# Front of a hybrid GLA / Gated DeltaNet layer: the last segment of four chunks is split into two of two chunks

## The chip, the cores and the metric

The kernel runs on one core of a Trainium2 chip. The metric is device microseconds from the start to the end of one execution, as the median of several runs. The engines are named as in the profile: PE (TensorE), DVE (VectorE), ACT (ScalarE), POOL (GpSimd), and SP (SyncE), which issues most DMAs.

## The reference, cut to what matters

One decoder layer on 2048 tokens of width 1024: a token mixer with two head groups, an output projection with a layer norm, then a mixture of 64 experts with top-2 routing and a second layer norm. The change touches the mixer alone.

```python
proj = x @ w_in                                   # 1024 x 3608
qa, ka, va, ra, lra, qb, kb, vb, zb, bb, ab = split(proj)
gk  = log_sigmoid(lra @ w_gk_up + b_gk) / 16
o_a = rms_norm(gla_chunked(qa, ka, va, gk)) * silu(ra)
q, k, v = split(silu(causal_conv(concat(qb, kb, vb))))   # 4 taps along the sequence
beta, g = sigmoid(bb), -exp(a_log) * softplus(ab + dt_bias)
o_b = rms_norm(gdn_chunked(l2(q), l2(k), v, beta, g)) * silu(zb)
x1  = layer_norm(alpha * x + concat(o_a, o_b) @ w_out)
```

Both groups carry a state from chunk to chunk. The kernel uses chunks of 128 tokens, 16 in all.

## The kernel before, in words

The mixer has two parts. The front (`mixer_front`) works through the 16 chunks in segments, `SEGS` in line 320, each a pair of first chunk and number of chunks.

`project(si)` (lines 366 to 399) multiplies the segment's tokens by all of `w_in`. It first turns the tokens (PE transposes, line 378) and splits them into a high and a low part, `xhi` and `xlo`, of which there is one buffer each. Then it goes through 14 blocks of 256 to 272 columns of `w_in`. Every block is loaded in four pieces `raw` (line 390, issued by SP, three buffers), cast to `whi` on ACT (line 392), and subtracted to `wlo` on DVE and POOL in turn (line 393). Six blocks are token-major (line 412): per chunk 24 matmuls with 256 moving columns. Eight are channel-major (line 440): twice 24 matmuls whose moving columns are the tokens of the segment, 512 for four chunks. Six of these eight feed the causal convolution: ACT copies the tile from PSUM to `cr` (line 452, one buffer), POOL moves the three-token halo (lines 453 and 454), DVE makes four steps (lines 455 and 457), ACT a tanh (line 459) and DVE a last step (line 460). Results go to DRAM. The PSUM tiles of all this are called `mm`, and there are two.

The main loop (lines 734 to 747) calls for each segment `segment_gates` (once per segment: some 30 small DVE steps, `Gates.segment`), then for each chunk `load`, `gla_pre`, `gdn_prep`, `gla_post`, and for the chunk four before it `scan.chunk`, which is the serial part of the delta rule; after every fourth chunk comes `solve`, a triangular solve of four chunks on POOL (62 dependent steps, lines 688 and 690), and then the next segment's `project`. `scan.chunk` takes its PSUM from tiles named `p`, for chunks from 12 on from `mm` (line 743); it takes eleven one after the other. Its own buffers in SBUF (pool `p3work`) are single. `E` is a work tile with two buffers that `gla_pre`, `segment_gates` and `solve` share.

The loop is written in this order, but a planner sets the order on each engine. Work that stands earlier in the text has priority; later work, such as the next segment's projection, fills what is free. So `project(si + 1)` runs beside the chunks of segment `si`. Each engine then executes its own list in order. Almost all DMAs go through SP's list, one behind the other.

The second part, `mixer_out`, splits `w_out` into `wohi` and `wolo` (lines 881 and 882), in memory that the projection's ring used, runs the last four scans and projects chunk by chunk (transposes in line 907, matmuls in line 919). Its first transposes use the PSUM of `mm`. The experts and the last layer norm follow.

Of the kernel before, what the change touches and what calls it, by code (L numbers as in the profile page):

```python
# [316 lines left out]
KW, RB = 2, 3  # L317
LAG = 4
LEVELS = (64, 32, 16, 8, 4, 2, 1)
SEGS = ((0, 4), (4, 4), (8, 4), (12, 4))  # L320


def mixer_front(tc, nc, gt, scan, ident, x, w_in, conv_w, gla_g, gdn_g, w_gk, b_gk, dr):


    with ExitStack() as es:
# [39 lines left out]
        def project(si):  # L366
            c0, nch = SEGS[si]
            nt = nch * 128
# [96 lines left out]
        def segment_gates(si):  # L465
            c0, nch = SEGS[si]
            gt.segment(nc, work, ps, c0, nch)
            gs = work.tile([128, 4, 256], F32, name="gseg", bufs=1)
            u = work.tile([128, 2, 8, 128], F32, name="E").rearrange(
                "p a b c -> p (a b c)")[:, :1024].rearrange("p (a b) -> p a b", a=4)  # L470
            for j in range(nch):
                pz = ps.tile([128, 4, 128], F32, name="z", bufs=1).rearrange("p a b -> p (a b)")
                nc.tensor.transpose(pz[:16, 256:384], lra[:, si % 2, j, :], ident)
                nc.vector.tensor_copy(lT[j % 2][:16, :], pz[:16, 256:384])
                z = pz[:, :256]
                nc.tensor.matmul(z, lT[j % 2], wgk, start=True, stop=True)
                nc.vector.tensor_scalar(gs[:, j, :], z, 0.0, None, op0=OP.min)
                nc.vector.scalar_tensor_tensor(u[:, j, :], gs[:, j, :], -2.0, z, op0=OP.mult, op1=OP.add)
                T["g", c0 + j] = gs[:, j, :]
            gs, u = gs[:, :nch, :], u[:, :nch, :]  # L480
            nc.scalar.activation(u, u, AF.Exp, scale=-1.0)
            nc.scalar.activation(u, u, AF.Ln, bias=1.0)
            nc.vector.tensor_sub(gs, gs, u)
# [188 lines left out]
        def solve(seg):  # L672
            XR = work.tile([128, 2, 8, 128], F32, name="E").rearrange("p a b c -> p a (b c)")
            X = XR[:64, 0].rearrange("p (a b) -> p a b", a=32)
            for b in range(4):
                nc.gpsimd.dma_start(
                    X[16 * b:16 * b + 16],
                    flat(dr["na"], [[128 * 128, 16], [128, 32], [1, 32]],
                         seg * 16 * 128 * 128 + 32 * b * 129))
            R = XR[:64, 1].rearrange("p (a b) -> p a b", a=32)  # L680
            nc.gpsimd.memset(R, 0.0)
            nc.gpsimd.affine_select(R, R, pattern=[[1, 32], [-1, 32]], compare_op=OP.not_equal,
                                    fill=1.0, base=0, channel_multiplier=0)
            tmp = work.tile([128, 256], F32, name="stmp", bufs=1)
            for j in range(31):
                m, w = 31 - j, j + 1
                tv = tmp[:64, :m * w].rearrange("p (a b) -> p a b", b=w)
                nc.gpsimd.tensor_mul(tv, X[:, j, j + 1:, None].to_broadcast([64, m, w]),  # L688
                                     R[:, j:j + 1, :w].to_broadcast([64, m, w]))
                nc.gpsimd.tensor_add(R[:, j + 1:, :w], R[:, j + 1:, :w], tv)  # L690
            RT = X
            nc.scalar.activation(RT, R.rearrange("p a b -> p b a"), AF.Copy)
            for i, r in enumerate((R, RT)):
                for b in range(4):
                    nc.gpsimd.dma_start(
                        flat(dr["td"], [[4096, 16], [1, 1024]],
                             (i * NT + seg * 4) * 4 * 4096 + b * 1024),
                        r[16 * b:16 * b + 16].rearrange("p a b -> p (a b)"))
# [34 lines left out]
        nc.vector.tensor_copy(lm, lmf)  # L733
        for si, (c0, nch) in enumerate(SEGS):
            segment_gates(si)
            for c in range(c0, c0 + nch):
# [7 lines left out]
                if c % 4 == 3:  # L744
                    solve(c // 4)
            if si + 1 < len(SEGS):
                project(si + 1)
# [923 lines left out]
```

## Time and profile before

| | |
|---|---|
| runs of the kernel before | 2542.12, 2557.68 and 2557.61 us, median 2557.61 |
| profiled execution | 2542.03 us, span from first to last instruction 2540.0 us |
| mean granted TensorE clock | 0.98 of 2.4 GHz |
| busy share of the span | PE 95%, DVE 66%, ACT 44%, POOL 31% |
| front: first projection matmul to last scan | from 22 to 1094 us |
| output projection | from 1094 to 1391 us |

Times in the rows are microseconds from the start of the span, unless ns is said. "Busy" of an engine is the time in which at least one of its instructions is under way. Matmuls overlap their neighbours, so the duration of one is longer than the time between two of them.

A row of a window gives the stretch A:B, its length, then for PE, PEld (weight loads), DVE, ACT and POOL the busy time with the number of instructions, then the granted TensorE clock as a share of 2.4 GHz, the DMA share and GB/s. A window of one line has only that line's engines.

### The profile page before, as it was taken

To read this page: it belongs to the slowest core of one execution; us is meant where nothing else is said; L and a number is where in the kernel's file an instruction comes from. 1 tells how busy PE (TensorE), PEld (TensorE's weight loads), DVE (VectorE), ACT (ScalarE), POOL (GpSimd) and SP (SyncE) were. 2 spreads that over 40 slices of the span, in tenths; PEclk is the share of its full clock that TensorE was granted. 3 is DMA by queue.
4 is the path that set the end of the run, shared out by engine and by line. 5 is a ranking of instruction groups with operands and counts; after the bars stand their busy time and mean duration, and the time that the engine had idled before them with its cause. 6 is when DMAs were issued, how large, how long until landed. Compare 5 with 4: busy or idle time off the path is not lost.

```text
span 2540.0 us, 44666 instructions
## 1 busy us (share of the span) xinstructions
PE 2401.4 (95%) x16115; PEld 1794.8 (71%) x16115; DVE 1672.7 (66%) x3814; ACT 1114.7 (44%) x2202; POOL 794.6 (31%) x967
## 2 busy tenths in 40 slices
PE   7999989999999989889998999999989999999978
PEld 6797769887888778778877466766657667666543
DVE  6746884778577865878887366746645667465537
ACT  3435443554464444622222255645544556455422
POOL 5222582234832482274222111211111111121106
PEclk9999999999999999999999999999999999999989
DMA  5466446555654555645364999999999999999978
GB/s 164 127 188 189 121 112 190 183 150 162 215 175 134 162 174 168 208 128 191 112 235 145 401 408 420 372 401 406 406 409 384 409 407 407 398 400 409 403 284 341
DMA packets 268853, 679.33 MB, mean 267 GB/s; under 512 B 44436, under 2 KB 163798, under 8 KB 217302
## 3 DMA queue, kind: packets, MB, share of 16 engines
q1 hardware_dynamic: 252470, 639.04, 68.7%
q0 software_dynamic: 15744, 36.76, 4.1%
q8 instruction: 128, 2.10, 0.3%
q14 instruction: 95, 0.78, 0.1%
q10 hardware_dynamic: 416, 0.66, 0.1%
HBM read 591.91 MB, written 98.08 MB: 272 GB/s over the span
## 4 chain that ended last, share of the span: by engine, by line
PE 50%; DMA 18%; DVE 8%; issue 3%; ACT 3%; POOL 2%; DVEq 0%; SPq 0%; POOLq 0%; ACTq 0%
DMA w<-in_w_experts_dram 16%; PE gu L1354 14%; PE y L919 7%; PE mm L412 6%; PE y L1354 6%; PE mm L440 3%; PE ysum L1605 2%; DVE w L1218 2%; DVE oa L457 1%; PE misc L943 1%; POOL E L690 1%; PE xt L1355 1%; POOL stmp L688 1%; PE e L543 1%; ACT w L1217 1%
## 5 line engine op out<-in xcount | busy, mean ns | idle before, releaser
L1354 PE MATMUL gu<-w,xh 128*128 128x512 f32 (+1 forms) x2144 | 561.0, 495 | 19.3 <-DVE w L1218 9.4
L1218 DVE TENSOR_TENSOR w<-w,w 128x2048 fp32r<-128x2048 f32 x192 | 435.5, 2287 | 153.3 <-ACT w L1217 124.8
L1217 ACT ACTIVATE w<-w 128x2048 fp32r<-128x2048 f32 x192 | 364.5, 1914 | 199.6 <-PE gu L1354 80.5
L1354 PEld LDWEIGHTS gu<-w,xh 128*128 128x128 f32 (+1 forms) x2144 | 284.9, 166 | 229.3 <-issue 145.2
L1454 POOL DMA_INDIRECT y_d<-xg,ids x52 | 94.4, 1816 | 711.4 <-ACT w L1217 309.9
L1354 PE MATMUL y<-w,hh 128*128 128x512 f32 (+1 forms) x1072 | 280.4, 495 | 9.6 <-DVE w L1218 6.4
L412 PE MATMUL mm<-whi,xhi 128*128 128x256 f32 (+2 forms) x768 | 225.9, 294 | 2.4 <-DVE xlo L383 1.1
L440 PE MATMUL mm<-xhi,whi 128*128 128x512 f32 x512 | 210.3, 411 | 18.4 <-ACT cr L452 18.1
L412 PE MATMUL mm<-whi,xlo 128*128 128x256 f32 (+2 forms) x768 | 220.1, 287 | 0.0
L412 PE MATMUL mm<-wlo,xhi 128*128 128x256 f32 (+2 forms) x768 | 219.9, 286 | 0.0
L1354 PEld LDWEIGHTS y<-w,hh 128*128 128x128 f32 (+1 forms) x1072 | 141.1, 166 | 104.7 <-issue 67.3
L393 POOL TENSOR_TENSOR wlo<-raw,whi 128x512 fp32r<-128x512 f32 (+2 forms) x112 | 151.1, 1349 | 203.0 <-ACT whi L392 200.6
L440 PE MATMUL mm<-xlo,whi 128*128 128x512 f32 x512 | 208.3, 407 | 0.0
L392 ACT ACTIVATE whi<-raw 128x512 fp32r<-128x512 f32 (+2 forms) x224 | 132.5, 628 | 169.2 <-DMA raw<-in_w_in_dram 111.1
L440 PE MATMUL mm<-xhi,wlo 128*128 128x512 f32 x512 | 206.2, 403 | 0.0
L1354 PE MATMUL gu<-w,xl 128*128 128x512 f32 x560 | 176.7, 396 | 0.0
L393 DVE TENSOR_TENSOR wlo<-raw,whi 128x512 fp32r<-128x512 f32 (+2 forms) x112 | 103.0, 926 | 98.0 <-ACT whi L392 96.5
L412 PEld LDWEIGHTS mm<-whi,xhi 128*128 128x128 f32 x768 | 146.1, 190 | 7.5 <-DVE xlo L383 1.5
L412 PEld LDWEIGHTS mm<-whi,xlo 128*128 128x128 f32 x768 | 145.9, 190 | 2.3 <-issue 1.2
L412 PEld LDWEIGHTS mm<-wlo,xhi 128*128 128x128 f32 x768 | 146.1, 190 | 1.0 <-issue 0.2
L1451 DVE SCALAR_TENSOR_TENSOR xg<-y,gate,xg 128x512 f32<-128x512 f32 x104 | 74.6, 746 | 93.3 <-PE y L1354 93.0
L457 DVE SCALAR_TENSOR_TENSOR oa<-cr,cw,oa 128x512 f32<-128x512 f32 x144 | 131.6, 914 | 3.2
(461 smaller groups left out, 4623.8 us busy)
## 6 DMA issues: line engine op xcount, KB each, us to landing
w<-in_w_experts_dram SPq DMA_DIRECT2D x384, 1024.0 KB, 21.5
raw<-in_w_in_dram SPq DMA_DIRECT2D x192, 256.0 KB, 3.1
y<-y_d SPq DMA_DIRECT2D x16, 1024.0 KB, 18.3
bT_d<-oa SPq DMA_DIRECT2D x48, 256.0 KB, 2.4
bT<-bT_d SPq DMA_DIRECT2D x16, 768.0 KB, 5.6
xt<-in_x_dram SPq DMA_DIRECT2D x32, 256.0 KB, 4.0
qk<-bT_d SPq DMA_DIRECT2D x16, 512.0 KB, 4.2
x<-in_x_dram SPq DMA_DIRECT2D x16, 512.0 KB, 4.0
```

The source lines that it names most:

```text
L392: nc.scalar.activation(hi[:, ks, :n], raw, AF.Copy)
L393: (nc.gpsimd if h % 2 else nc.vector).tensor_sub(lo[:, ks, :n], raw, hi[:, ks, :n].bitcast(F32))
L412: nc.tensor.matmul(p[:, :n], xs[:, k, j * 128:(j + 1) * 128], ws[:, k, :n], start=(m == 0), stop=(m == 3 * KD - 1))
L440: nc.tensor.matmul(p, ws[:, k, s * 128:(s + 1) * 128], xs[:, k, :nt], start=(m == 0), stop=(m == 3 * KD - 1))
L457: nc.vector.scalar_tensor_tensor(o, r[:, w:w + nt], cw[:, w, b:b + 1], o, op0=OP.mult, op1=OP.add)
L919: nc.tensor.matmul(pf, a[:, k, :], w[:, k, cs], start=(m == 0), stop=(m == 3 * KD - 1))
L1217: self.nc.scalar.activation(full(hi), full(raw), AF.Copy)
L1218: self.nc.vector.tensor_sub(full(lo), full(raw), full(hi).bitcast(F32))
L1354: mm = lambda *args, **kw: tc.keep_in_program_order(nc.tensor.matmul(*args, **kw))
L1451: nc.vector.scalar_tensor_tensor(yt[:, cs], py[j], col.gate[:, c:c + 1], yt[:, cs], op0=OP.mult, op1=OP.add)
L1454: put = nc.gpsimd.indirect_dma_start(out=y_d, out_offset=bass.IndirectOffsetOnAxis(ap=col.ids[r, c:c + 1], axis=0), in_=yt[r], in_offset=N ...
L1605: keep(nc.tensor.matmul(p[:, cs], ident, ys[t][:, i, cs], start=(i == 0), stop=(i == 1)))
```

## The change

One line. The last segment, chunks 12 to 15, becomes a segment of chunks 12 and 13 and one of chunks 14 and 15. There are then five calls of `project`, the last two with 256 tokens each, and five of `segment_gates`; `project(4)` stands in the loop behind chunk 13 and before chunk 14. `solve` keeps its place behind every fourth chunk, and line 743 its limit of chunk 12.

```diff
--- before.py
+++ after.py
@@ -317,7 +317,7 @@
 KW, RB = 2, 3
 LAG = 4
 LEVELS = (64, 32, 16, 8, 4, 2, 1)
-SEGS = ((0, 4), (4, 4), (8, 4), (12, 4))
+SEGS = ((0, 4), (4, 4), (8, 4), (12, 2), (14, 2))
 
 
 def mixer_front(tc, nc, gt, scan, ident, x, w_in, conv_w, gla_g, gdn_g, w_gk, b_gk, dr):
```

## Rows read from the trace of the kernel before

**Rows 1.** The page, part 1: engine, busy us (share of the span), instructions.

```profile
PE 2401.4 (95%) x16115; PEld 1794.8 (71%) x16115; DVE 1672.7 (66%) x3814; ACT 1114.7 (44%) x2202; POOL 794.6 (31%) x967
```

**Rows 2.** Windows of the front, all engines (columns: see above).

```profile
454.00:715.00 261.00, 255.11 (x2404) 218.10 (x2391) 189.82 (x575) 131.12 (x411) 125.25 (x182) 0.99 0.60 181
715.00:988.00 273.00, 259.36 (x2474) 222.49 (x2472) 192.34 (x590) 126.98 (x398) 120.33 (x176) 0.95 0.52 153
988.00:1094.00 106.00, 91.85 (x1391) 73.91 (x1390) 85.00 (x365) 63.72 (x253) 31.55 (x53) 0.90 0.68 209
988.00:1042.00 54.00, 46.84 (x711) 37.87 (x714) 41.80 (x152) 34.92 (x126) 16.35 (x26) 0.87 0.78 244
1042.00:1094.00 52.00, 45.01 (x697) 36.05 (x684) 43.20 (x214) 28.80 (x129) 15.19 (x27) 0.93 0.58 172
```

**Rows 3.** The chain of waits, 840 to 990 us: start, length, what, how many.

```profile
917.37 19.44 PE mm L440 x72
...
972.81 3.03 PE mm L412 x24
```

**Rows 4.** Single lines: count: ns min/median/max, first and last start.

```profile
L845 PE MATMUL p<-gdn_s,qk x64: 275/275/275, 480.7 to 896.9; 128*128 128x128 f32 x64
...
L845 PE MATMUL mm<-gdn_s,qk x32: 275/288/421, 1016.6 to 1091.4; 128*128 128x128 f32 x32
...
L907 PE MATMUL mt<-ident,ma x64: 271/273/328, 1094.5 to 1352.0; 128*128 128x128 f32 x64
```

**Rows 5.** Windows of the channel-major line 440 and the token-major line 412 alone.

```profile
60.00:85.00 25.00, 24.24 (x103) 18.80 (x103) 1.00 0.43 123
842.00:936.00 94.00, 73.79 (x288) 54.97 (x289) 0.96 0.54 155
...
165.00:202.00 37.00, 35.87 (x288) 34.25 (x287) 1.00 0.58 176
```

**Rows 6.** Single lines 412 and 440.

```profile
L412 PE MATMUL mm<-whi,xlo x768: 274/283/689, 22.7 to 988.3; 128*128 128x256 f32 x128, 128*128 128x272 f32 x32, 128*128 128x264 f32 x32
...
L440 PE MATMUL mm<-xhi,whi x512: 387/393/796, 49.7 to 935.9; 128*128 128x512 f32 x171
```

**Rows 7.** Lines by form, 715:988 us: count | busy us, mean ns | idle before.

```profile
L392 ACT ACTIVATE whi<-raw 128x512 fp32r<-128x512 f32 x48 | 28.3, 626 | 30.7 <-DMA raw<-in_w_in_dram 20.1 <-PE mm L440 7.7 <-PE mm L412 2.7
...
L393 DVE TENSOR_TENSOR wlo<-raw,whi 128x512 fp32r<-128x512 f32 x24 | 21.3, 892 | 22.2 <-ACT whi L392 22.2
...
L393 POOL TENSOR_TENSOR wlo<-raw,whi 128x512 fp32r<-128x512 f32 x24 | 32.8, 1367 | 29.4 <-ACT whi L392 27.3 <-POOL att L574 1.1 <-ACT gu L286 1.0
```

**Rows 8.** Single lines of VectorE.

```profile
L457 DVE SCALAR_TENSOR_TENSOR oa<-cr,cw,oa x144: 730/752/2470, 58.4 to 924.2; 128x512 f32<-128x512 f32 x144
...
L424 DVE SCALAR_TENSOR_TENSOR st<-th,st x64: 404/426/1596, 28.4 to 989.7; 128x256 f32<-128x256 f32 x64
...
L293 DVE SCALAR_TENSOR_TENSOR gp<-gp,gs x7: 157/166/174, 820.3 to 825.1; 128x16 f32<-128x16 f32 x7
```

**Rows 9.** Single line 390, the weight loads on SP's queue, 715 to 988 us.

```profile
L390 SPq DMA_DIRECT2D raw<-in_w_in_dram x49: 368/383/777, 714.9 to 964.8; - x49
```

**Rows 10.** Windows of smaller stretches, columns as in rows 2.

```profile
715.00:744.00 29.00, 25.56 (x514) 22.05 (x512) 22.60 (x77) 16.14 (x51) 9.73 (x14) 0.82 0.54 161
...
842.00:875.00 33.00, 33.00 (x180) 26.12 (x179) 30.27 (x84) 17.27 (x54) 13.68 (x17) 1.00 0.53 160
883.00:941.00 58.00, 50.82 (x248) 40.81 (x247) 41.57 (x69) 24.02 (x50) 48.97 (x77) 0.94 0.54 160
```

**Rows 11.** Lines of VectorE in 842:875 and 883:941 us.

```profile
L457 DVE SCALAR_TENSOR_TENSOR oa<-cr,cw,oa 128x512 f32<-128x512 f32 x12 | 9.2, 765 | 0.1
...
L457 DVE SCALAR_TENSOR_TENSOR oa<-cr,cw,oa 128x512 f32<-128x512 f32 x12 | 14.8, 1232 | 0.1
```

**Rows 12.** Lines, 988 to 1094 us.

```profile
L882 DVE TENSOR_TENSOR wolo<-x,wohi 128x1024 fp32r<-128x1024 f32 x8 | 10.4, 1308 | 1.4 <-ACT wohi L881 1.4
```

## Prediction, written before the changed kernel ran

> **What bounds the kernel now.** I read the page's busy times first, then the windows of the front's stretches, then the chain of waits and single lines. TensorE is busy 95% of the span and VectorE 66% [rows 1], but those shares mix stages, and the change touches only the front (everything before the output projection), so it has to be read there. The windows cut the front where a projection's last matmul ends. The third segment's chunks with the last projection beside them take 273 us, and the last four chunks, with no projection left, 106 us [rows 2]. The change works on these 379 us. The reader is to see two things. First, the bare 106 us are not empty: TensorE is busy 91.85 of them, so 14.2 us are idle, at a mean granted clock of 0.90, against 0.95 and 0.99 in the stretches with a projection [rows 2]. The first half of them (chunks 12 and 13) idles 54 - 46.84 = 7.2 us at 0.87, the second half (chunks 14 and 15) 52 - 45.01 = 7.0 us at 0.93. Second, a projection does not come free beside chunks: 261 and 273 us go by with TensorE idle only 5.9 and 13.6 us [rows 2]. The time is the sum of both works, not the longer one. The chain inside the channel-major blocks goes through VectorE's convolution as well as TensorE (72 matmuls in 19.44 us, 0.27 us each, slower than when nothing holds them), and through TensorE alone in the token-major blocks (24 in 3.03 us) [rows 3]. The front ends with the scan: its four bare chunks read the state from 1016.6 to 1091.4 us, one per 25 us, and the output projection's first transposes follow at 1094.5 [rows 4].
>
> **The matmuls.** A projection has 8 channel-major blocks x 2 x 24 = 384 matmuls of 512 columns and 576 token-major ones. Two half projections have 768 of 256 columns instead of the 384, and the same 576. For the price I take instructions per time and not durations: 103 matmuls of 512 columns fill 24.24 us, 0.2353 us each; 288 of 256 columns fill 35.87 us, 0.1246 us each [rows 5]. So 768 x 0.1246 - 384 x 0.2353 = 95.7 - 90.4 = **+5.3 us**. The last token-major tiles, 24 in 3.03 us [rows 3], would make it +6.6; exact halving 0; I keep 0 to 7. The durations say otherwise: 283 ns against 393 ns [rows 6], and 768 x 0.283 - 384 x 0.393 would be +66 us. But neighbours overlap, as the counts per time show, so that is no price here. The Trainium skill (Trainium Kernel Development and Optimization, Performance Expectations) warns that matmul busy time misleads on how close a kernel is to its limit, because matmuls are pipelined. By the busy times the sum would be 61 us higher; the counts side with the Trainium skill.
>
> **Chunks 12 and 13 get cover.** Their 7.2 us of idle fall to the rate of the two covered stretches, (5.9 + 13.6)/534 = 3.7% of some 47 us, 1.7 us: **-5.5 us** (0 to -7.2). The clock: at 0.87, 2 x 0.13 x 54 = 14 us of that half ran at 1.2 GHz, at 0.97 it would be 3. Eleven microseconds at full pace save at most half, 5.5; but the scan's matmuls had a median of only 288 ns there against 275 elsewhere [rows 4], so I take **-2.5 us** (0 to -5.5). Chunks 14 and 15 stay bare, and their 7.0 us of idle stay.
>
> **A second pass over the input weights.** One more projection loads and splits all of them again, 14 blocks of 4 pieces: 56 ScalarE casts at 626 ns, 35 us; 28 subtractions on VectorE at 892 ns, 25 us; 28 on GpSimd at 1367 ns, 38 us [rows 7]. The convolution and its neighbours become twice as many half-width steps. The nearest row for a 256-wide three-operand step on VectorE is 426 ns, against 752 for 512 wide [rows 8], so 36 steps cost 36 x (2 x 426 - 752) = 3.6 us more, and the two steps around them some 2.4 more by the same ratio. A fifth round of gate arithmetic is 26 short steps like the 166 ns one [rows 8], 4.3 us. Together VectorE gets about 35 us more on 192.3 + 85.0 = 277.3 of 379 us [rows 2], which makes 82%. On SP's queue there are 56 more weight loads at 383 ns [rows 9], 21 us of issue, and each waits for a buffer of `raw` with the chunk loads, stores and scan loads queued behind it. All of it lies beside TensorE's work as long as the chunks fill TensorE; VectorE has run at 30.27 of 33 us, 92%, with TensorE not idle at all [rows 10]. Where the solve on GpSimd meets the convolution that cover is gone: 7.2 of 58 us idle [rows 10]. Twelve of the last projection's sixteen channel tiles took 94 us [rows 5]; sixteen at half the columns are 94 x 16/12 / 2 = 63 us, and 12.4% of that is **+7.8 us**. Bounds: 0 with full cover, +35 with none of VectorE's added time covered. I take the value by the solve row because project(4)'s channel blocks must start soon after that solve.
>
> GpSimd's added work has a second price. A convolution step takes 765 ns where GpSimd is lightly used and 1232 ns beside the solve [rows 11]. If all 38 us of added GpSimd work met such steps, they would lose 38 x (1 - 765/1232) = 14 us; that stands inside the bound above. The Trainium skill (GPSIMD Engine Reference, Key points) gives a reason against the change: GpSimd shares its SBUF interfaces with VectorE and contends with instructions that read two SBUF inputs. The two rows agree; without that rule the added GpSimd work would cost VectorE nothing.
>
> **One more start.** project(4) can write `xhi` only after project(3)'s last matmul, as every projection must. The last such start shows 25.56 of 29 us busy [rows 10]: 3.4 us idle, and chunks beside it. Half the tokens are turned each time, so no transpose is added. I take **+1.5 us** (0 to 3.4).
>
> **The output weights move.** The split of `w_out` needs memory of the projection's ring, so it now waits for project(4) and falls beside chunks 14 and 15. It is 8 VectorE subtractions, 10.4 us [rows 12], in a stretch where VectorE is already busy 43.2 of 52 us [rows 2]: 53.6 us of work. The output projection uses the slices one after the other, so only a part is late: **+3 us** (0 to 10.4).
>
> **Sum.** 5.3 - 5.5 - 2.5 + 7.8 + 1.5 + 3 = **+9.6 us**. On the profiled execution's 2542.0 us (span 2540.0) that is 2551.6. The runs shown stand at two levels, 2542.1 once and 2557.7 and 2557.6; with the profiled one their mean is 2549.9, and I put the change on that mean: **2559.5 us**. All the bounds together are -13 to +56, but the ends exclude each other: full cover goes with the gains, no cover with the losses. One per cent, about what a measurement of this kernel can tell from no change, is 25 us, so the forecast is no change.
>
> **Rivals.**
> *Slower: the scan loses its buffers.* For chunks from 12 on the scan takes its PSUM from `mm`, of which there are two. Before, no projection was left then; now project(4) takes from the same two, with 4 turns, 16 channel tiles and 12 token tiles against 11 takes per scan chunk. If scans 8 and 9 are put off until project(4) is through, four scans stand in the bare end, 4 x 25 = 100 us [rows 4], instead of 52. TensorE has then its 45 us of chunks 14 and 15 and some 16 of the two scans (an estimate, a third of 45), so 39 us are idle instead of 7: 32 us more, 2591.5. With one scan late it is half, 2575.5. It decides from the point where both scans stand behind project(4)'s last tile. For it: the scan is a serial chain, and bare it already sets the pace of 25 us. Against it: the covered scans between 480.7 and 896.9 us [rows 4] kept up in the planner's order. Chance 0.13.
> *A little faster: the solve moves off the convolution.* project(3) ends earlier, so the third solve may meet its token blocks and project(4)'s start instead of the channel blocks. Then the 7.2 us idle of 883 to 941 go away and +7.8 becomes -7.2: sum -5.4, 2544.5. For it: the solve hangs on chunk 11 alone. Against it: the solve is some 58 us long and project(4) begins inside it. Chance 0.17.
> *It does not do what it says.* Chunk 12 needs project(3)'s last blocks, the gates and an `E` buffer that the solve also holds; if chunks 12 and 13 therefore come mostly after project(4), the -5.5 and -2.5 are gone: +17.6, 2567.5. Chance 0.12.
> Forecast: 0.58.
>
> **How the numbers follow.** The forecast's own range is 2545.5 (both gains in full, feed and start at nothing: 5.3 - 7.2 - 5.5 + 3 = -4.4) to 2569 (the feed twice as dear and the start at 3.4: +19.3). Below lies the second rival on the lower of the two levels of the runs, above it the first: 2534 to 2586 leaves out most of the two-scan case. Slower by over 1% (above 2575) needs both scans late or most of the added VectorE time bare: 0.10 + 0.04 = 0.14. Faster by over 1% needs more than the 14 us of bare idle and clock that chunks 12 and 13 have to give: 0.03. The rest, 0.83, is no change.
>
> **What would show it.** The bare end, from the last projection matmul to the output projection, should be 50 to 60 us instead of 106, at a clock like 0.93. From 715 us to that point it should be some 325 to 340 instead of 273. VectorE busy in the whole stretch should be near 312 us and GpSimd 40 higher. The 256-column matmuls of the channel blocks should come about 0.125 us apart. If the four reads of the state in `mm` still lie 25 us apart and end 75 us after the first, with the first near the end of project(4), the first rival holds. A front that ends before 1080 us would mean that the feed is hidden; the time after the front should move with its end and not change by itself.

## The result and the profile after

The changed kernel takes 2661.84 us (median of 4 runs, 2656.95 to 2672.62), beside 2555.70 us for the kernel before (4 runs): a ratio of 1.043, 95% interval 1.038 to 1.047. It is 106 us slower where no change was forecast. The profiled execution after took 2656.95 us, its span 2655.1. The medians of the kernel before that were taken beside the experiments lie between 2547.83 and 2556.24 us, so a few microseconds between kernels of different experiments are not read as a difference.

Up to the end of the third projection both kernels run the same instructions in the same order. The profiled one after is 13.5 us later by then (726.7 against 713.2 us); the runs of the kernel before differ among themselves by as much. From there to the output projection's first transposes the kernel before takes 381.3 us and the changed one 478.6. What follows is nearly equal: 2540.0 - 1094.5 = 1445.5 us against 2655.1 - 1205.3 = 1449.8. So the whole loss lies in the stretch that the change touches. The page's first part, beside [rows 1], shows TensorE 46 us busier and GpSimd 40:

```profile
PE 2447.1 (92%) x16505; PEld 1846.9 (70%) x16505; DVE 1727.2 (65%) x3929; ACT 1155.1 (44%) x2295; POOL 834.4 (31%) x1019
```

Windows after, columns as in [rows 2]: the fourth projection beside chunks 8 to 11; then a stretch with no projection; the fifth projection; the bare end:

```profile
728.00:925.00 197.00, 176.97 (x2112) 159.98 (x2112) 155.00 (x524) 106.46 (x364) 82.00 (x119) 0.91 0.62 183
925.00:1028.00 103.00, 62.69 (x736) 49.67 (x735) 56.85 (x195) 34.96 (x133) 49.75 (x85) 0.67 0.34 103
1028.00:1151.00 123.00, 100.99 (x839) 94.52 (x839) 80.95 (x192) 57.53 (x141) 40.98 (x50) 0.94 0.56 163
1151.00:1205.00 54.00, 43.74 (x593) 34.96 (x592) 41.68 (x156) 30.72 (x109) 16.10 (x22) 0.84 0.64 206
```

The second line is the failure of the change's purpose. Most of chunks 12 and 13 still runs with no projection beside it: TensorE idles 40.3 of 103 us, and its granted clock is 0.67, two thirds of the time at 1.2 GHz. The third line is the other loss: half a projection, with the fifth round of gates and some work of chunk 14 beside it, takes 123 us, where the whole first one of the kernel before takes 181. The last line is the bare end for chunks 14 and 15, half as long as the 106 us of [rows 2].

The chain of waits after, 925 to 1155 us (start, length, what), tells why nothing covers the second line:

```profile
989.44 3.45 POOL td_d L695 x7
992.89 2.24 DMA td_d<-E
995.28 1.89 DMA td<-td_d
997.31 1.26 POOL tt L786
...
1025.20 1.71 PE mm L845 x8
1026.91 1.68 PE mm L769 x8
1029.06 3.62 DMA xt<-in_x_dram
```

And TensorE's waits in 925 to 1028 us (engine, line, what it waited for: us, times, longest):

```profile
PE mm L800 <- DMA td<-td_d: 13.8, 1, 13.8
PE e L543 <- DVE E L523: 10.0, 3, 6.8
```

Scan 8 takes its PSUM tiles from `mm` and waits for the third solve, which stores its result at 989 to 995 us. The `mm` tiles are handed out in the order of the program's text, and there scans 8 and 9 (called with chunks 12 and 13) stand ahead of the fifth projection. So its input load and transposes come directly behind scan 9's last matmuls at 1027 us, 102 us after the projection before it ended. The scan's reads in `mm` after, beside [rows 4]:

```profile
L845 PE MATMUL mm<-gdn_s,qk x32: 275/348/421, 1008.8 to 1203.6; 128*128 128x128 f32 x32
```

Before, the four reads lay within 75 us, behind all projections. Now two lie ahead of the last projection and two behind it, 195 us from first to last.

### The profile page after: what moved, and what is told of

Read it like the earlier page. It is cut to its first block, busy times and chain, and to the rows that moved or that the text cites. A ratio compares the mean times of both kernels' runs of the same rounds, so it can differ in the third digit from the quotient of the medians.

```text
span 2655.1 us, 45942 instructions
## 1 busy us (share of the span) xinstructions
PE 2447.1 (92%) x16505; PEld 1846.9 (70%) x16505; DVE 1727.2 (65%) x3929; ACT 1155.1 (44%) x2295; POOL 834.4 (31%) x1019
## 4 chain that ended last, share of the span: by engine, by line
PE 41%; DMA 25%; DVE 10%; ACT 4%; issue 3%; POOL 2%; SPq 0%; DVEq 0%; ACTq 0%; POOLq 0%
DMA w<-in_w_experts_dram 21%; PE gu L1354 11%; PE y L919 6%; PE mm L412 4%; PE y L1354 4%; PE mm L440 3%; DMA raw<-in_w_in_dram 3%; PE ysum L1605 2%; DVE w L1218 2%; DVE oa L457 1%; PE misc L943 1%; ACT whi L392 1%; DVE wlo L393 1%; POOL E L690 1%; PE xt L1355 1%
## 5 line engine op out<-in xcount | busy, mean ns | idle before, releaser
L393 POOL TENSOR_TENSOR wlo<-raw,whi 128x512 fp32r<-128x512 f32 (+2 forms) x140 | 189.2, 1352 | 290.6 <-ACT whi L392 289.8
L440 PE MATMUL mm<-xhi,whi 128*128 128x512 f32 (+1 forms) x640 | 238.8, 373 | 28.4 <-ACT cr L452 28.2
L392 ACT ACTIVATE whi<-raw 128x512 fp32r<-128x512 f32 (+2 forms) x280 | 166.9, 630 | 207.2 <-DMA raw<-in_w_in_dram 145.2
L440 PE MATMUL mm<-xlo,whi 128*128 128x512 f32 (+1 forms) x640 | 234.2, 366 | 0.0
L440 PE MATMUL mm<-xhi,wlo 128*128 128x512 f32 (+1 forms) x640 | 233.2, 364 | 0.0
L393 DVE TENSOR_TENSOR wlo<-raw,whi 128x512 fp32r<-128x512 f32 (+2 forms) x140 | 124.3, 893 | 110.2 <-ACT whi L392 107.8
L440 PEld LDWEIGHTS mm<-xhi,whi 128*128 128x128 f32 x640 | 127.9, 200 | 55.1 <-ACT cr L452 34.6
L440 PEld LDWEIGHTS mm<-xhi,wlo 128*128 128x128 f32 x640 | 128.2, 200 | 17.8 <-issue 0.2
```

Source lines behind the costliest of these rows:

```text
L392: nc.scalar.activation(hi[:, ks, :n], raw, AF.Copy)
L393: (nc.gpsimd if h % 2 else nc.vector).tensor_sub(lo[:, ks, :n], raw, hi[:, ks, :n].bitcast(F32))
L440: nc.tensor.matmul(p, ws[:, k, s * 128:(s + 1) * 128], xs[:, k, :nt], start=(m == 0), stop=(m == 3 * KD - 1))
```

## Experiments: the scans' buffers

**Scans 8 and 9 in p.** The changed kernel, where only the scans behind the last projection take `mm`:

```diff
-  name="mm" if c >= 12 else "p", bufs=2))
+  name="mm" if c >= 14 else "p", bufs=2))
```

(The `c` of this line is the chunk with which a scan is called, four ahead of its own: `c >= 12` is scan 8 onward. Where the expectations speak of scans 12 and 13, they mean those called with these chunks, scans 8 and 9.)

> The changed kernel with one number altered: the scan takes its PSUM from mm only for chunks 14 and 15, and from p for chunks 12 and 13. Theory A (the two mm buffers): in the changed kernel project(4) got its first mm tile only when scan 9 had taken its last, so it ran alone after chunks 12 and 13. Then project(4)'s transposes should start within some 20 us of project(3)'s last matmul, the bare end should stay near 54 us, and the time should fall from 2657 to 2550 to 2575 us (my forecast of +9.6 on before). Theory B (the second pass over the weights at half width is dear wherever it runs): the time stays above 2620 us, with project(4) still taking over 110 us for itself. Theory C (scan 8 waits for the third solve): the 13.8 us wait of TensorE for td stays and the time falls by less than 20 us.

Measured: 2614.37 us, ratio 1.024 (1.022 to 1.027). The fifth projection now starts 2 us after the fourth (927.0 after 924.8), and 47 us of the 106 are back. The time lies between the ranges of theory A (2550 to 2575) and theory B (above 2620): each has a part of the loss. The rest, some 60 us, is not a matter of this order. Windows of this kernel, and of the kernel before over the same stretch of work, from the third projection's end to the output projection:

```profile
725.00:1164.00 439.00, 370.50 (x4285) 329.38 (x4284) 336.73 (x1071) 231.41 (x749) 188.03 (x275) 0.90 0.59 177
```

```profile
713.00:1094.00 381.00, 353.21 (x3893) 297.93 (x3891) 278.11 (x956) 192.25 (x654) 152.16 (x229) 0.94 0.56 168
```

In 58 us more, TensorE is busy 17 us more and idle 41 us more (68.5 against 27.8), VectorE is busy 59 us more, GpSimd 36, ScalarE 39. The two largest of TensorE's waits in these stretches (us, times, longest), first here, then in the kernel before:

```profile
PE mm L440 <- ACT cr L452: 16.1, 8, 4.6
PE e L543 <- DVE E L523: 13.9, 7, 5.6
```

```profile
PE mm L440 <- ACT cr L452: 6.5, 2, 5.0
PE e L543 <- DVE E L523: 3.5, 5, 1.1
```

The first hangs on the convolution's buffer, the second on a step that VectorE makes for each chunk. Together they are 20 of the 41 us of added idle time; the rest is spread over many short waits.

**The same hole made in the kernel before.** Scan 4 onward takes `mm`, so that the whole last projection stands behind scan 7:

```diff
-  name="mm" if c >= 12 else "p", bufs=2))
+  name="mm" if c >= 8 else "p", bufs=2))
```

> The kernel before, segments of four, with the scan taking mm already for chunks 8 to 11. Theory A: project(3) now waits until scan 7 has taken its last mm tile, so chunks 8 to 11 run bare (some 106 us) and the whole project(3) alone (some 182 us) instead of both in 273 us: 15 to 30 us slower than before, 2560 to 2585, because a whole projection alone is not much slower than TensorE and the third solve lies beside it. If the loss of cover alone explains the changed kernel's 97 us, it should be 60 us or more here. Theory B: no projection is added, so no more than 10 us slower.

Measured: 2587.90 us, ratio 1.013 (1.011 to 1.016), 34 us slower. The last projection begins at 831.2 us, right behind scan 7, and its matmuls then take 182.5 us nearly alone. That is 3 us above theory A's range. Two `mm` tiles claimed too early cost 34 us with no half projection anywhere.

**A short third solve.** The changed kernel with 4 of the third solve's 31 steps; the other 27 are left out:

```diff
-  for j in range(31):
+  for j in range(4 if seg == 2 else 31):
```

> The changed kernel with the third solve cut to its first 4 of 31 steps (27 steps of the triangular solve for chunks 8 to 11 are left out, so later values differ, and only the front is read). Theory C (scan 8, and behind it project(4), wait for that solve on GpSimd): the wait for td goes away and the front ends 25 to 45 us earlier than in the changed kernel's 1205 us. Theory A alone, without the solve: it ends no more than 15 us earlier. Theory B: no change over 10 us.

Measured in one run: 2617.34 us; the output projection begins at 1167.6 instead of 1205.3 us, 38 us earlier, as theory C had it. TensorE's wait for `td` is gone, and the stretch without a projection shrinks from 101 to 53 us. This kernel also has less work on GpSimd, so the 38 us need not all come from the shorter wait. The loss is one chain, solve to scan 8, scan 9, `mm`, projection; broken at the first link it gives back 38 us, at `mm` 47.

## Experiments: what a projection of two chunks costs

**The first segment in two.** The kernel before, where `mm` has no other taker so early:

```diff
-SEGS = ((0, 4), (4, 4), (8, 4), (12, 4))
+SEGS = ((0, 2), (2, 2), (4, 4), (8, 4), (12, 4))
```

> The kernel before with the first segment of four chunks split into two of two, the last left whole; no scan runs there, so mm is free for the projection. Theory A (the two mm buffers are what costs): the second pass is then hidden beside chunks 0 and 1, and the time is 2542 to 2575 us. Theory B (half-width passes are dear by themselves): the first projection, alone and for two chunks, takes 115 us or more instead of half of the 182 us that a whole one alone takes, and the second one is as slow: 40 to 100 us slower than before, above 2590.

Measured: 2630.40 us, ratio 1.030 (1.028 to 1.032). So a second pass over the weights costs 77 us where no scan takes `mm`, within theory B's range. The first projection of two chunks, and the whole first projection of the kernel before:

```profile
15.00:143.00 128.00, 106.04 (x838) 99.33 (x837) 81.75 (x180) 59.10 (x135) 54.49 (x72) 0.91 0.60 178
```

```profile
22.00:203.00 181.00, 174.02 (x1098) 150.68 (x1099) 104.67 (x207) 67.69 (x144) 48.53 (x62) 0.99 0.52 152
```

Half the columns take 71% of the time. VectorE, ScalarE and GpSimd do 78%, 87% and 112% of a whole pass's work for them, since casts and subtractions of the weights don't get shorter. TensorE's waits in the two:

```profile
PE mm L440 <- ACT cr L452: 13.5, 10, 2.4
PE mm L412 <- DVE lra L426: 2.8, 1, 2.8
```

```profile
PE mm L440 <- ACT cr L452: 5.7, 3, 2.2
```

Ten pauses instead of three. Five of the ten were followed by a stretch at half clock; the other five, 0.3 to 2.4 us long, were not. Line 440 alone in e3_split_first, 2 us inside each of three tiles: the first follows a pause of 1.9 us, the second one of 0.3 and the third one of 2.4 (last columns: granted clock, DMA share, GB/s):

```profile
68.50:70.50 2.00, 2.00 (x11) 2.00 (x11) 0.50 0.72 222
72.00:74.00 2.00, 2.00 (x19) 2.00 (x19) 1.00 0.74 192
103.00:105.00 2.00, 2.00 (x20) 2.00 (x19) 1.00 0.62 152
```

By their start times a matmul of 256 columns follows the last after 0.21 us at 1.2 GHz and after 0.12 at 2.4.

**One shared cause after another.** Two theories for the pauses were a single `cr` buffer under the convolution, and weights that come late:

```diff
-  xt = ring.tile([128, 512], F32, name="xt", bufs=3)
+  xt = ring.tile([128, 512], F32, name="xt", bufs=2)
...
-  r = ring.tile([128, 515], F32, name="cr", bufs=1)
+  r = ring.tile([128, 515], F32, name="cr", bufs=2)
```

> The kernel before with its first segment as two of two chunks (as in e3_split_first, which took 2630.4 us), and a second cr buffer for the convolution; to make room, two xt buffers instead of three. Theory D (the convolution's chain over one cr buffer sets the pace of a projection of two chunks): in e3_split_first TensorE started a weight block of the convolution every 9.9 us (six of them in a pass of 128 us), where its 48 matmuls need 6.0 at 0.125 us; with a second buffer the pitch falls to what VectorE needs, 2 x (0.43 + 3 x 0.59 + 0.63) + 2 x 0.84 = 7.3 us, so 2.5 us x 12 blocks = 30 us less: 2600 (2590 to 2612). Theory F (the weights arrive too late: three raw buffers, the DMA, the split): no change, 2625 to 2635. Theory V (VectorE's own work sets the pace): 2620 to 2632.

Measured: 2612.34 us, ratio 1.023 (1.019 to 1.026): 18 us less, 30 expected, at the upper end of theory D's range. The waits for `cr` go from 13.5 to 7.4 us in the first pass, and a wait of 6.5 us for `oa` takes some of their place.

With `RB = 4` in place of the second `cr`:

> The kernel before with its first segment as two of two chunks (as in e3_split_first, 2630.4 us), and four raw buffers for the weights instead of three; two xt buffers instead of three. Theory D (the convolution's one cr buffer): within 8 us of 2630. Theory F (the weights arrive too late; in the first pass ScalarE waited 27.1 us in 23 waits for raw): 10 to 40 us less, 2590 to 2620. Theory V (VectorE's own work): within 5 us of 2630.

Measured: 2635.57 us, 1.030 (1.026 to 1.034). A fourth `raw` buffer gives nothing.

With three of the four loads of each weight block left out in the projections of two chunks:

```diff
-  raw = ring.tile(...); nc.sync.dma_start(raw, ...)
+  if h == 0 or nch == 4:
+      raw = ring.tile(...); nc.sync.dma_start(raw, ...)
```

> The kernel before with its first segment as two of two chunks (as e3_split_first, 2630.4 us), where the projections of two chunks load only the first of the four pieces of each weight block and split it four times: it leaves out three quarters of their weight loads (and so computes those products from the wrong weights), with every split, matmul and eviction kept. Theory J (two chains of about one length, the convolution over one cr buffer and the weights' way from the SyncE queue through three raw buffers; either alone hides most of the other's removal): 10 to 30 us less, 2600 to 2620, as the second cr buffer alone gave 18. Theory D (the cr chain alone): 2620 to 2632. Theory V (the splits' own work on ScalarE, VectorE and GpSimd): 2622 to 2635.

Measured: 2599.94 us, 1.017 (1.013 to 1.022), 30 us less, at the lower end of theory J's range. Both in one:

> As g1_split_cr2 (2612.3 us: first segment in two, two cr buffers, two xt buffers), with three quarters of the weight loads of the projections of two chunks left out as in g5_split_one_raw. Theory J: with both chains shortened TensorE runs nearly unbroken, some 95 us a pass instead of 116 and 122, so 25 to 50 us less: 2562 to 2588. Theory V (the splits' own work sets the pace once cr is doubled): 2600 to 2612. Theory D alone: 2600 to 2615.

Measured: 2589.07 us, 1.0145 (1.011 to 1.018). That is 23 us below g1_split_cr2, 1 us above theory J's range and clear of the others'; the 18 and the 30 make 41 together, and 37 us against the kernel before (ratio 1.0145) remain with both chains shortened.

Neither helps the change itself, whose two projections run beside chunks. The kernel of e1_scan_in_p with a second `cr`:

> The changed kernel with scans 12 and 13 in p (as e1_scan_in_p, 2614.4 us), and a second cr buffer, with two xt buffers instead of three. Theory D: both projections of two chunks gain up to 2.5 us in each of 6 blocks where no chunk work fills the gap, so 10 to 30 us less in all, 2585 to 2604, still above the kernel before. Theories F and V: 2608 to 2622.

Measured: 2615.96 us, 1.023 (1.020 to 1.027). And with three of four loads left out:

> The changed kernel with scans 12 and 13 in p (e1_scan_in_p, 2614.4 us), with three quarters of the weight loads of its two projections of two chunks left out. Theory J: 10 to 40 us less, 2575 to 2604: the repeated loads are then the larger part of what is left over before beside the cr chain. Theories D and V: 2604 to 2618: the remaining 60 us are then in the chunk work, which a narrower projection leaves less TensorE time to lie beside.

Measured: 2610.80 us, 1.023 (1.019 to 1.027). So neither change is worth anything here by itself: theory D fails with the first, theory J with the second. The two in one kernel, which together gave 41 us in e3_split_first, were not tried in this place. In the kernel before, a second `cr` changes nothing either:

> The kernel before with a second cr buffer and two xt buffers instead of three. Theory D: its six convolution blocks start every 12.84 us beside no chunk where 48 matmuls of 512 columns take 11.3, so up to 1.5 x 6 = 9 us less in the first projection and somewhat less in the three beside chunks: 5 to 20 us less than before, ratio 0.992 to 0.998. Theories F and V: within 4 us of before.

Measured: 2560.64 us, 1.0017 (1.0002 to 1.0032).

**The work on the weights and the convolution.** What was left was VectorE's added 59 us. First all subtractions of the low parts on GpSimd, in the two projections of two chunks of e1_scan_in_p:

```diff
-  (nc.gpsimd if h % 2 else nc.vector).tensor_sub(
+  (nc.gpsimd if h % 2 or nch == 2 else nc.vector).tensor_sub(
```

> The changed kernel with scans 12 and 13 in p (e1_scan_in_p, 2614.4 us), with all the low-part subtractions of the weights in its two projections of two chunks on GpSimd: 56 instructions of 0.84 us leave VectorE, 47 us, and GpSimd gets them at 1.34 us, 75 us on top of 188 in 439. Theory V (VectorE is what these 60 us are: from the end of the third projection to the first addition of the output it is busy 337 us in e1_scan_in_p and 278 in the kernel before, +59, where the stretch grew by 57): 20 to 45 us less, 2570 to 2594. Theory K (TensorE: a projection of half the time covers less of the chunk work, and the clock falls in the gaps): within 10 us, 2604 to 2624, or slower where GpSimd's four subtractions in a row, 5.4 us, come late for a block of 6 us.

Measured: 2659.29 us, 1.041 (1.039 to 1.043), 45 us slower, against theory V and as theory K allowed. VectorE hardly gets emptier by it:

```profile
730.00:1208.00 478.00, 389.29 (x4279) 344.71 (x4278) 328.76 (x1014) 229.81 (x747) 245.05 (x329) 0.85 0.55 163
```

Its 337 us became 329, though instructions of 45 us left it. Part of that is seen in its convolution steps: line 457's took 48.2 us instead of 41.5, line 455's 18.3 instead of 10.3. So this kernel doesn't tell VectorE's load from the lateness of four subtractions in a row. Then three of the four taps of the convolution left out in the two projections:

```diff
-  for w in range(1, 4):
+  for w in range(1, 4 if nch == 4 else 1):
```

> As e1_scan_in_p (2614.4 us), with three of the four taps of the convolution left out in the projections of two chunks: 72 instructions of 0.59 us, 42 us, leave VectorE, and the chain over the cr buffer gets 1.8 us shorter per turn (which g3_e1_cr2 showed to be worth nothing here). Theory V: 15 to 40 us less, 2574 to 2600. Theory K: within 10 us, 2604 to 2620.

Measured: 2592.88 us, 1.016 (1.014 to 1.018), 21.5 us less for 41.5 us of steps on VectorE, within theory V's range. Both of these in one:

> h1_e1_split_pool and h2_e1_one_tap in one: VectorE loses 89 us of 337 and is busy less than in the kernel before. Theory V: 40 to 65 us less than 2614.4, 2550 to 2575, close to the kernel before. Theory K: 2595 to 2620.

Measured: 2650.71 us, 1.037 (1.034 to 1.040). Both theories missed, V by 75 us and K by 31. VectorE is down to 288 us of work there and the kernel is still 97 us slower than before, so VectorE's load alone doesn't set the time. What h1_e1_split_pool and this kernel share is the subtractions on GpSimd; that these govern is the likely reading, not one that was tested. In the kernel before, moving them all to GpSimd costs too:

> The kernel before with all the low-part subtractions of the weights on GpSimd: 112 instructions of 0.89 us, some 100 us, leave VectorE in the front, and GpSimd gets four of 1.37 us in a row, 5.5 us, for a weight block of 11 to 13 us. Theory V, if VectorE is a second bound of the front of the kernel before too: 5 to 30 us faster. Theory K: within 6 us, or slower by up to 30 where the chunks' own work on GpSimd stands behind the subtractions.

Measured: 2584.34 us, 1.012 (1.010 to 1.014).

Last, the subtractions left out altogether in the two projections (which then take no `wlo` tile either), with TensorE's work kept:

```diff
+  if nch == 4:
       (nc.gpsimd if h % 2 else nc.vector).tensor_sub(lo[...], raw, hi[...])
-  passes = ((xhi, hi), (xlo, hi), (xhi, lo))
+  passes = ((xhi, hi), (xlo, hi), (xhi, lo if nch == 4 else hi))
```

> As e1_scan_in_p (2614.4 us), with the low-part subtractions of the weights left out in the projections of two chunks; the third matmul of each triple multiplies by the high part again, so TensorE's work is unchanged and the low parts of the weights are left out of those products. VectorE loses 47 us and GpSimd 75. Theory W (the repeated preparation of the weights, ScalarE to VectorE and GpSimd, is what TensorE's pauses follow from): 25 to 50 us less, 2564 to 2590. Theory K (a narrow projection covers too little, whatever stands beside it): 2602 to 2620.

Measured: 2569.55 us, 1.006 (1.004 to 1.008): 45 of the 60 us are gone, within theory W's range. But this leaves out more than the change had added: 45 us of subtractions on VectorE and 74 on GpSimd, where the repeated pass had added 22 and 37. The kernel before with the same left out of its last projection was not run. And with the three taps left out as well:

> j1_e1_no_low, with three of the four taps of the convolution left out as well in the projections of two chunks (h2_e1_one_tap: 2592.9 us). Theory W with VectorE as the shared engine: the two add up, 2545 to 2572, at most 20 us above the kernel before. Theory K: 2580 to 2600, no more than h2_e1_one_tap gave.

Measured: 2553.61 us, 0.9995 (0.998 to 1.002): the time of the kernel before. The two kernels' windows over the same stretch of work, columns as in [rows 2]:

```profile
724.00:1121.00 397.00, 360.90 (x4278) 321.96 (x4277) 258.61 (x1016) 229.07 (x748) 108.92 (x223) 0.92 0.65 199
```

```profile
716.00:1093.00 377.00, 353.73 (x4281) 316.67 (x4279) 224.75 (x937) 227.92 (x748) 109.45 (x221) 0.93 0.67 206
```

The stretch from the third projection's end to the output projection follows the median time through all of these:

```
kernel                stretch us  TensorE idle  VectorE busy   median
before                   381.3        27.8         278         2555.7
changed                  478.6        92.6         335         2661.8
e1_scan_in_p             438.6        68.5         337         2614.4
h1_e1_split_pool         478.1        88.7         329         2659.3
h2_e1_one_tap            412.9        47.2         302         2592.9
h3_e1_both               467.9        78.9         288         2650.7
j1_e1_no_low             397.5        36.1         259         2569.6
j2_e1_no_low_one_tap     377.7        23.3         225         2553.6
```

So the 106 us go in three steps: 47 with the order of the `mm` tiles, 45 with the subtractions of the low parts in both narrow projections, and 16 with three of their four convolution taps. The last two steps take away more work than the change had added; they show what the 60 us hang on, not how they divide. Note that j2_e1_no_low_one_tap has VectorE emptier than the kernel before and is no faster: it shows that the loss is gone without this work, not that the change gains anything once it is. Which share of the 45 us is VectorE's time, and which is GpSimd standing in its way or the low parts coming late, is not told apart: leaving the subtractions out removes all three. No kernel without left-out work was found that beats the kernel before.

## Why the prediction was wrong

*The order of the work.* The forecast let chunks 12 and 13 get cover (-5.5 and -2.5 us). They got none: 40.3 us idle and a clock of 0.67. The first rival named the right resource, the two `mm` tiles, and turned the queue round: it put scans 8 and 9 behind the projection, where in fact the projection stood behind them. It took its price, 32 us, from TensorE's work in the bare end, and its chance, 0.13, from scans that had kept up in `p`, whose tiles they share with no projection. The sign of its price was right; e1_scan_in_p and e6_mm_from_8 measured 47 and 34 us. The third rival had chunks 12 and 13 come uncovered, as they did, but by another mechanism and on the wrong side of the projection, at +17.6 us. What decided was in the code and in [rows 4] together: the takes of `mm` stand in program order, and scan 8 can't begin before the third solve. I read the order but priced only the scans' delay by the projection.

*The second pass.* This is the term that failed by most: +7.8 us, bounded at +35. e1_scan_in_p, where chunks 12 and 13 do get cover, is still 61 us above the kernel before, which leaves some 59 for this term if the others were right. Three steps of it were off. (1) The cover. "All of it lies beside TensorE's work as long as the chunks fill TensorE" took a stretch at 92% of VectorE with TensorE not idle [rows 10] for the rule. There a tile is 512 columns wide and gives VectorE and GpSimd 24 x 0.2353 = 5.6 us; at 256 columns it gives 3.0, and the work on the weights keeps its length. e3_split_first shows this with no solve and few chunks beside it. (2) The upper bound. It was VectorE's added time, 35 us. The engine's busy time grew by 59 (335 us in the changed kernel, 312 forecast): the split is 22 of it, the convolution 14 (6 forecast), the fifth round of gates 8 (4.3 forecast), and most of the rest are the chunks' own steps, which got longer; line 522's 56 steps went from 19.4 to 26.6 us. A lower clock of TensorE, 0.90 against 0.94, came on top. (3) The width. I priced a 256-wide convolution step at 426 ns from another line [rows 8]. It measured 485 at the median of e3_split_first's first pass, of which 66 to 76 us are shown, and 577 on average in e1_scan_in_p:

```profile
L457 DVE SCALAR_TENSOR_TENSOR oa<-cr,cw,oa 128x256 f32<-128x256 f32 x6 | 2.9, 485 | 0.2
```

Two of them take 970 ns against 752 for the 512-wide one. Over the whole stretch line 457 took 41.5 us, against 33.9 in the kernel before: 7.6 more, 3.6 forecast. The Trainium skill (VectorE: DVE Perf Modes, the section on the TRN2 errata) says that a large tile pays the latency between instructions once and small tiles pay it each, and to tile at 512 or more. These rows agree; the prediction had the effect in its sum, but sized it from another line.

*What held, and what can't be told.* The matmuls: at full clock, 256 columns start every 0.12 us, as forecast; TensorE's 17 us of added busy time in e1_scan_in_p go with a clock of 0.90 instead of 0.94, so the +5.3 can't be read off by itself. The bare end: 54 us, 50 to 60 forecast, though at a clock of 0.84 and not 0.93. GpSimd's work in the stretch: 189 - 152 = 37 us, 40 forecast. The output weights (+3): the time behind the front grew by 4.3 us, but in the kernels here, which differ in the front alone, it lies anywhere from 1445.5 to 1455.4, so the term is not shown. The start (+1.5) was not measured by itself. The sum could not hold: from the third projection's end to the last one's, 728 to 1151 us, it is 423 us, 325 to 340 forecast, and the time stands far above the range.

The second rival, a solve that moves off the convolution, did not show: a gain of 7 us can't be seen beside losses of this size.

## What to carry to other kernels

Before a segment is cut, ask which work per pass does not shrink with it, and whether the engine that hides it still has the time per tile; here each weight block's split had 11 us of matmuls to lie behind, and after the change 6. And follow each shared buffer pool in program order: a tile claimed early by a step that must wait for something slow holds back everything that comes later to the same pool, however ready it is.

## What the runs showed of the hardware

Some of VectorE's steps get longer when GpSimd does more beside them. The same 256-wide convolution step over the whole stretch, first in j1_e1_no_low (no subtraction on GpSimd in these projections; two more lines ahead, so line 457 is 459), then in e1_scan_in_p (74 us of them), then in h1_e1_split_pool (141 us):

```profile
L459 DVE SCALAR_TENSOR_TENSOR oa<-cr,cw,oa 128x256 f32<-128x256 f32 x72 | 36.4, 506 | 1.3
```

```profile
L457 DVE SCALAR_TENSOR_TENSOR oa<-cr,cw,oa 128x256 f32<-128x256 f32 x72 | 41.5, 577 | 1.0
```

```profile
L457 DVE SCALAR_TENSOR_TENSOR oa<-cr,cw,oa 128x256 f32<-128x256 f32 x72 | 48.2, 670 | 1.5
```

506, 577 and 670 ns: moving VectorE's work to GpSimd gave a part of it back. The Trainium skill (GPSIMD Engine Reference, Key points) names the shared SBUF interfaces and VectorE instructions with two SBUF inputs, as these are. Line 457's rows agree and give the size that I had put inside a bound. Other steps with two such inputs do not follow: line 460's take 604 and 603 ns on average in the last two kernels, line 522's 474 and 392.

The other surprise was TensorE's clock after short pauses. In the first pass of e3_split_first TensorE is idle 22 of 128 us, with no wait over 2.8 us, and the mean granted clock is 0.91, so some 23 us went by at 1.2 GHz; in the kernel before it is idle 7 of 181 us, at 0.99. Yet a pause of 2.4 us at 102 us left the clock at 1.00, and one of 1.9 us at 67 us was followed by 0.50.
